# Hybrid backbone step on one core: gates' bias tile, early RWKV loads, token tiles to DRAM, and the order of the last attention units

## The chip, the cores and the metric

The kernel runs on one NeuronCore of a Trainium2 chip. The metric is device time of one execution in microseconds (us), lower is better. Time before: 2095.14 us, the median of 3 runs (2094.40 to 2097.18).

## The reference

One inference step of a two-layer backbone, for 256 prompt tokens and 1024 latent tokens that share the weights (model width 1024, 10 tiles of 128 tokens). Cut to what matters here:

```
h = rms_norm(x, g) * (1 + scale) + shift          # scale, shift, gate from SiLU(cond) @ mod_w + mod_b
layer 0: z = h @ w_in                              # 3584 columns
   A: q, k (normed, rotary), softmax attention: latents read 512 cached + 1024 own keys, prompt its own 256
   B: RWKV-7 scan, forward and backward, 8 heads of 64
   out = concat(A * silu(gate_a), (norm(B) + bonus) * silu(gate_b)) @ w_out
   x1 = x + gate * out
layer 1: z = h1 @ w_in -> gated linear attention (GLA), 4 heads, both directions
   y = final_norm(x1 + gate * (rms_norm(o) * silu(g)) @ w_out)
```

Products that need full precision are made of three products of rounded halves (high x high, high x low, low x high; `mm3`), so a tile of 128 tokens through the output projection is 2 halves of 512 columns with 24 products each.

## The kernel before, in words

The whole program is written by a planner, `Sched` (L104). Each piece of work is a Python generator, a task, that emits instructions with modelled costs; tasks come in streams, and `drive` (L411) takes at each step the instruction that could start earliest by the model, less the lead of its stream; on equal times the lower rank of the stream goes first, then the earlier task. The order that comes out is the order of each engine's queue on the chip, and each engine works its queue strictly in that order. Three details matter:

- A PE instruction that uses another size of the array than the one before it counts as 0.095 later (L296, `SWITCH`).
- A stream is given as (tasks, how many at once, share, lead, spare). With a share its rank begins at that of the RWKV stream and rises with the PE time that it has used; RWKV has share 2000, attention 150, the maxima 60 (L1793 to L1797).
- Buffers are counted slots: `get(tag)` waits until a slot of this name is free in the plan, `put` gives it back. `sch.until(...)` holds a task back in the plan; it makes no instruction.

All DMAs are issued on the SP queue.

Stages, in order of time:

1. *Layer-0 projections* (to about 510 us): `units`, `operands`, and eight gate units (`gated`, L785). A gate unit needs one of two `gt` buffers per group of tokens: PE's result, tanh on ACT, a product on DVE, a store to DRAM; then the buffer is free.
2. *Rooms.* SBUF is reused stage by stage. `room_attn` (L1239) opens the attention's tiles, loads the keys KA, and clears the lower half of both KB on GpSimd. `room_rwkv` (L1310) waits until the gate units are over and two PSUM banks are free, loads three masks, allocates and fills the RWKV tiles, and then sets the flag `rwkv`; only then do the segments (`rwkv_seg`, L1381) ask for their buffers and load AR, BK and Vs (three buffers each).
3. *Mixers* (about 515 to 1290): 40 RWKV segments, the attention in 12 units (p4, g): four pairs of heads times three groups of tokens, g = 0 the 256 prompt tokens (2 tiles of keys), g = 1 and 2 the 512 latents each (12 tiles of keys). The order of units is (1, 2, 0) for each p4 (L1668). `maxima` makes the row maxima of a unit ahead of it, at a pace tied to the units done (`want`, L1696), and writes them into row 64 of QB; `attend` makes the exponentials and the products with the values. `mods` (L1300) computes the remaining modulation columns with 1 MB of weights each; for the gate columns it takes a `gt` buffer for the bias row (`row` in `mod_cols`, L551, L565).
4. *Output projection of layer 0.* When all segments are over, `room_proj` (L2274) opens the output weights and two buffers each for `oh`, `ol` (halves of the input of a tile) and `xt`. `out_tile` (L2191) takes a tile of 128 tokens when all eight parts of its group's mixer output are in DRAM (four attention units, four RWKV norms): load through the single buffer `wst`, split, 48 products, gate, add to x, squares, store of x1 (L2256). It then waits for the flag `normed`, keeping its `xt`, and `norm_tile` (L621) scales `xt` in place, turns it with PE, and writes the layer-1 input. Order of tiles: groups 1, 2, 0. The gate row of a group is loaded into one buffer, which is free for the prompt's row when all eight latent tiles are over (L2214).
5. `room_norm` (L2281) sets `normed` when all 12 attention units, the modulation and the RWKV norms are over. Then the layer-1 projections may begin: `project` (L1805) loads weights through the same `wst` (`split_weights`, L655). Two gate units of layer 1 go first (`NGATE`); the GLA's rooms open when all ten tiles are normed.
6. *Layer 1*: projections, GLA, output projection (to 2093 us).

Of the kernel before, what the change touches and what calls it, by code (L numbers as in the profile page):

```python
# [20 lines left out]
P = 128  # L21
# [465 lines left out]
def tile_hybrid_dit_step(ctx: ExitStack, tc: tile.TileContext, I, C, O):  # L487
# [63 lines left out]
    def mod_cols(i, c0, n, bank, row, ready=lambda: True):  # L551
# [4 lines left out]
        for a in range(NK // nk):  # L556
            w = yield from get("mw", False)
            ws.append(w.rearrange("p a c -> p (a c)").rearrange("p (k c) -> p k c", c=n))
            D.dma_start(out=ws[a], in_=I["mod_w"][i, a * nk * P:(a + 1) * nk * P, c0:c0 + n].rearrange("(k p) c -> p k c", p=P))

            def loaded():
                mod_loads[0] += 1
            sch.then(loaded)
            if a == 0 and c0 >= 2 * DM:
                b = yield from get(row, False)  # L565
                D.dma_start(out=b[0:2, 0:n], in_=I["mod_b"][i:i + 1, c0:c0 + n].to_broadcast([2, n]))
# [9 lines left out]
        m4 = yield from get("m4", False)  # L576
        m = m4[:, 0:n]
        copy(m, p)
        if c0 < 2 * DM:
            k0 = c0 % DM // P  # L580
            ks = slice(k0, k0 + n // P)
            q = p[:, 0:2 * (n // P)].rearrange("p (k c) -> p k c", c=2)
            with sch.together():
                for k in range(n // P):
                    PE.matmul(q[:, k, :], lhsT=m[:, k * P:(k + 1) * P], rhs=msel, start=True, stop=True)
            wide = lambda r: par[:, r + ks.start:r + ks.stop].unsqueeze(2).to_broadcast([P, n // P, 2])
            to = gsh[i][:, 1 - c0 // DM, ks, :]
            V.tensor_tensor(to, q, wide(R_MB + i * 16 + c0 // DM * 8), ALU.add)
            if c0 >= DM:
                V.scalar_tensor_tensor(out=to, in0=to, scalar=1.0, in1=wide(R_NG + i * 8), op0=ALU.add, op1=ALU.mult)  # L590
        else:
            PE.matmul(p[0:2, :], lhsT=msel, rhs=m, start=True, stop=True)
            V.tensor_tensor(b[0:2, 0:n], p[0:2, :], b[0:2, 0:n], ALU.add)
            V.tensor_scalar(m[0:2, :], b[0:2, 0:n], 0.5, 0.0, ALU.mult, ALU.add)
            put(row, b)
            D.dma_start(out=gate_d[i][:, c0 - 2 * DM:c0 - 2 * DM + n], in_=m[0:2, :])
# [121 lines left out]
    flags = dict(left=0, gates=0, attn=False, keys=0, rwkv=False, mods=False, normed=False, gla=False, gl=False, units=0, weights=0, lr=0, begun=0, ra=False)  # L718
# [8 lines left out]
    shared("sq", 6, [P, 4])  # L727
# [12 lines left out]
    def layer0():  # L740
# [153 lines left out]
        def mods(n):  # L894

            yield from sch.until(lambda: loads[0] >= (5 if n % 2 else 1))
            yield from mod_cols(0, n * 512, 512, "a", "xr", lambda: modded[0] and modded[1])
# [341 lines left out]
    def room_attn():  # L1239
# [27 lines left out]
        for v in range(2):  # L1267
            G.memset(KB[v][64:128, :].bitcast(F32), 0.0)
            G.memset(KB[v][64:65, :].bitcast(F32), 1.0)
# [7 lines left out]
    def load_keys(v, x):  # L1277

        src = kh_d[64 * v:64 * v + 64, 0, :]
        if x == 0:  # L1280
            for h in range(2):
                D.dma_start(out=KA[v][64 * h:64 * h + 64, :].bitcast(F32), in_=kh_d[64 * v:64 * v + 64, h, :])
        else:
            D.dma_start(out=KB[v][0:64, :].bitcast(F32), in_=src)

    def keys():

        yield from sch.until(lambda: flags["attn"])
# [11 lines left out]
    def mods():  # L1300
        yield from sch.until(lambda: flags["attn"])
        for i, c0 in ((0, 2 * DM), (1, 0)):
            for c in range(c0, 3 * DM, 256):
                yield from mod_cols(i, c, 256, "b", "gt")
# [5 lines left out]
    def room_rwkv():  # L1310
# [15 lines left out]
        D.dma_start(out=m1f, in_=C["k_m1"].rearrange("p (d c) -> p d c", d=2))  # L1326
        id16 = rc.tile([P, P], F16, name="id16")
# [10 lines left out]
        slots("y", 2, [P, T], pool=rn)  # L1338
        slots("AR", 3, [P, 3, 4, 64])
        slots("BK", 3, [P, 2, 4, 64])  # L1340
        slots("Vs", 3, [P, 2, 2, 64])
# [326 lines left out]
    units = [(p4, g) for p4 in range(4) for g in (1, 2, 0)]  # L1668
# [120 lines left out]
    def attention(f):  # L1789
        for i, (p4, g) in enumerate(units):  # L1790
# [6 lines left out]
              (attention(attend), 2, 150), ([keys()], 1), ([mods()], 1))  # L1797
# [7 lines left out]
    def project(cols, use):  # L1805
        yield from sch.until(lambda: flags["normed"])
        yield from project_on(I["od_w_in"][0], H["hi"], H["lo"], cols, use, lambda g, a: normed[g] == GROUPS[g][1] // P, ORDER)
# [75 lines left out]
    def gates(h, u):  # L1883
# [13 lines left out]
        yield from project([(0, OD_G + unit * P, P)], use)  # L1897
# [293 lines left out]
    def out_tile(i, tt, src, finish):  # L2191
# [19 lines left out]
        put("wst", ot)  # L2211
        if i == 1:
# [7 lines left out]
        m = 256 if tt == 2 else 512  # L2220
# [30 lines left out]
    used = {}  # L2251
    NW1 = 2
    MIXED = (8, 4)

    def finish0(tt, xt, sq):
        D.dma_start(out=x1_d[tt], in_=xt)  # L2256
        yield from sch.until(lambda: flags["normed"])
# [4 lines left out]
        sch.then(done)  # L2262

# [10 lines left out]
    def room_proj():  # L2274
# [3 lines left out]
        slots_in(pool(left, "xr", side="left"))("xr", 1, [P, NK, P])  # L2278
# [75 lines left out]
    def tiles(i):  # L2354
        return ((out_tile(i, tt, (x_src, lambda t: x1_d[t])[i], (finish0, finish1)[i]) for tt in TILES), 3)

    def weights(i):
# [6 lines left out]
              weights(0), tiles(0), *gla, (projections(), 2, None, 0.0, 1.5), weights(1), tiles(1))  # L2364
# [85 lines left out]
```

## Time and profile before

| | us |
|---|---|
| median of 3 runs | 2095.14 |
| the profiled execution | 2095.28 |
| its span in the trace | 2093.5 |
| PE busy | 1997.0 (95%) |
| PE weight loads busy (beside the products) | 1557.7 (74%) |
| DVE busy | 1452.4 (69%) |
| ACT busy | 1007.6 (48%) |
| POOL (GpSimd) busy | 289.9 (14%) |
| DMA engines busy, mean share of the 16 | 33% |

The engine rows overlap in time; the span is the time from the first to the last instruction on the busiest path, and the run's time is 1.8 us more. Nearly every instruction carries line L357, the line of the planner that issues it, so instructions are told apart by the names of the tiles: `woh,oh` is a product of the output projection, `ident,xt` a transpose in `norm_tile`, `pt,VO` attention with the values, `QA,KA` and `QB,KB` scores, `KA,QA` maxima, `AR,BK` the first products of an RWKV segment. `pj` and `a` are PSUM banks. In brackets behind an instruction stands the time that its engine stood idle before it and what ended that.

### The profile page before, as it was taken

The numbers are of one execution on the slowest core, as the hardware profiler recorded it, in microseconds if no ns is written. First come the engines' busy times: TensorE is split into PE (matmuls) and PEld (weight loads), VectorE is DVE, ScalarE is ACT, GpSimd is POOL, SyncE is SP. The second block draws the span as 40 slices with busy tenths as digits, with TensorE's granted clock in tenths as the row PEclk, the third lists the DMA queues.
The fourth block names the chain that finished last, engine by engine and source line by source line (L and its number), as shares of the span: only waits on it lengthen the run. The fifth ranks groups of instructions, "written<-read, shape, count | busy, mean of one in ns | idle before, by whom it ended". The sixth has DMA issues, their size and how long they took to land.

```text
span 2093.5 us, 38539 instructions
## 1 busy us (share of the span) xinstructions
PE 1997.0 (95%) x14876; PEld 1557.7 (74%) x14876; DVE 1452.4 (69%) x2879; ACT 1007.6 (48%) x2184; POOL 289.9 (14%) x383
## 2 busy tenths in 40 slices
PE   6999999998999999999999999799999999999998
PEld 4878687886667777777776766578778888888886
DVE  4677866777887888778888987453575656564455
ACT  4454744553556655665656563333445454542111
POOL 2010200013221112121110020010121111110011
PEclk9999999999999999999999999899999999999999
DMA  8224342527513241323223224342102011115653
GB/s 297 71 101 159 138 164 81 179 91 238 170 54 103 81 143 59 97 74 111 78 68 88 67 70 143 95 146 73 50 14 64 28 50 29 49 31 165 192 170 112
DMA packets 215143, 219.56 MB, mean 105 GB/s; under 512 B 16480, under 2 KB 161232, under 8 KB 214960
## 3 DMA queue, kind: packets, MB, share of 16 engines
q1 hardware_dynamic: 214960, 217.10, 33.0%
q8 instruction: 117, 1.92, 0.4%
q14 instruction: 66, 0.54, 0.1%
HBM read 149.63 MB, written 67.39 MB: 104 GB/s over the span
## 4 chain that ended last, share of the span: by engine, by line
PE 52%; DVE 11%; issue 4%; ACT 3%; DMA 1%; POOL 0%; SPq 0%; POOLq 0%; DVEq 0%; ACTq 0%
PE a L357 26%; PE pj L357 26%; DVE QQ L357 2%; DVE LL L357 1%; DVE mx L357 1%; ACT QQ L357 1%; DVE TT L357 1%; DVE dec L357 1%; DVE gt L357 1%; DVE Z L357 1%; DVE y L357 1%; DVE GR L357 0%; DVE KX L357 0%; DVE GH L357 0%; DVE Ad L357 0%
## 5 line engine op out<-in xcount | busy, mean ns | idle before, releaser
L357 PE MATMUL pj<-hhi,whi 128*128 128x512 f32 (+1 forms) x672 | 241.1, 361 | 2.6 <-DVE whi L357 1.4
L357 PE MATMUL pj<-hhi,wlo 128*128 128x512 f32 (+1 forms) x672 | 240.4, 360 | 1.6 <-DVE wlo L357 1.6
L357 PE MATMUL pj<-hlo,whi 128*128 128x512 f32 (+1 forms) x672 | 241.3, 361 | 0.6 <-DVE hlo L357 0.6
L357 PEld LDWEIGHTS pj<-hhi,whi 128*128 128x128 f32 x672 | 128.9, 192 | 26.4 <-issue 3.7
L357 PEld LDWEIGHTS pj<-hhi,wlo 128*128 128x128 f32 x672 | 128.9, 192 | 24.0 <-issue 4.1
L357 PEld LDWEIGHTS pj<-hlo,whi 128*128 128x128 f32 x672 | 129.1, 192 | 23.7 <-issue 5.8
L357 POOL TENSOR_TENSOR acc<-acc,pt 128x512 f32<-128x512 f32 (+1 forms) x57 | 73.0, 1286 | 389.3 <-ACT pt L357 190.5
L357 PE MATMUL a<-h1hi,whi 128*128 128x512 f32 (+2 forms) x304 | 111.9, 369 | 0.0
L357 PE MATMUL a<-h1lo,whi 128*128 128x512 f32 (+2 forms) x304 | 111.0, 366 | 0.0
L357 PE MATMUL a<-h1hi,wlo 128*128 128x512 f32 (+1 forms) x296 | 109.9, 371 | 0.0
L357 PE MATMUL pj<-h1hi,whi 128*128 128x512 f32 (+2 forms) x296 | 108.4, 366 | 1.5 <-ACT h1hi L357 0.8
L357 PE MATMUL pj<-h1lo,whi 128*128 128x512 f32 (+2 forms) x296 | 108.4, 366 | 0.0
L357 PE MATMUL pj<-h1hi,wlo 128*128 128x512 f32 (+1 forms) x280 | 102.4, 366 | 0.0
L357 DVE TENSOR_TENSOR acc<-acc,pt 128x512 f32<-128x512 f32 (+1 forms) x127 | 90.6, 736 | 14.4 <-ACT pt L357 9.5
L357 PE MATMUL a<-pt,VO 128*64 128x512 f32 (+1 forms) x368 | 95.9, 605 | 0.0
L357 POOL TENSOR_SCALAR sq<-sq 128x1 f32<-128x1 f32 x70 | 19.9, 284 | 510.2 <-ACT gt L357 225.1
L357 DVE TENSOR_REDUCE mx<-pj 128x1 f32<-128x512 f32 (+1 forms) x118 | 75.4, 653 | 3.3 <-PE pj L357 3.1
L357 DVE TENSOR_REDUCE mx<-a 128x1 f32<-128x512 f32 x90 | 59.1, 669 | 10.8 <-PE a L357 10.7
L357 ACT ACTIVATE pt<-pj 128x512 f32<-128x512 f32 (+1 forms) x105 | 60.8, 597 | 10.2 <-PE pj L357 7.8
L357 PE MATMUL pj<-woh,oh 128*128 128x512 f32 (+1 forms) x160 | 61.5, 384 | 3.9 <-DVE oh L357 3.9
L357 PEld LDWEIGHTS a<-h1hi,whi 128*128 128x128 f32 (+1 forms) x304 | 56.9, 187 | 9.5 <-DVE gt L357 0.8
L357 PEld LDWEIGHTS pj<-h1hi,whi 128*128 128x128 f32 (+1 forms) x296 | 55.5, 188 | 11.2 <-ACT h1hi L357 1.2
(509 smaller groups left out, 5477.0 us busy)
## 6 DMA issues: line engine op xcount, KB each, us to landing
mw<-in_mod_w SPq DMA_DIRECT2D x24, 1024.0 KB
ws<-wk SPq DMA_DIRECT2D x32, 512.0 KB
wst<-in_ev_w_in SPq DMA_DIRECT2D x26, 512.0 KB
wst<-in_od_w_in SPq DMA_DIRECT2D x24, 512.0 KB
AR<-ws SPq DMA_DIRECT2D x40, 256.0 KB
BK<-ws SPq DMA_DIRECT2D x40, 256.0 KB
wst<-o SPq DMA_DIRECT2D x14, 512.0 KB
Vs<-vt SPq DMA_DIRECT2D x80, 64.0 KB
```

The lines of the kernel that those rows point to most:

```text
L357: r = f(*a, **k)
```

## The change

- `mod_cols` no longer takes a `gt` (or `xr`) buffer for the bias row: it takes `m4` earlier and puts the bias into its second half.
- `room_rwkv` allocates y, AR, BK and Vs ahead of the other RWKV tiles and sets a new flag `segs`; the segments load on `segs` and wait for `rwkv` only behind their loads. KB and VO (`keys`) are loaded after `segs`. The lower half of each KB is cleared on VectorE, where its upper half is loaded.
- The last pair of heads has the unit order (0, 1, 2), and the last two units are a stream of their own without share and with lead 0.15.
- Layer-0 token tiles go in the order 0 to 9 (prompt first). Tiles from 4 on wait ahead of their products until all steps of keys of all units are made. A tile that is over before `normed` gives its `xt` back after the store of x1; `renorm` loads x1 again later and norms it. `sq` has 12 slots in place of 6, `xr` 2 in place of 1.
- Layer-1 projections wait until eight token tiles have been split; the two early gate units take the groups in the order 0, 1, 2.

```diff
@@ mod_cols
             if a == 0 and c0 >= 2 * DM:
-                b = yield from get(row, False)
-                D.dma_start(out=b[0:2, 0:n], in_=I["mod_b"][i:i + 1, c0:c0 + n].to_broadcast([2, n]))
+                m4 = yield from get("m4", False)
+                b = m4[0:2, n:2 * n]
+                D.dma_start(out=b, in_=I["mod_b"][i:i + 1, c0:c0 + n].to_broadcast([2, n]))
...
@@ room_attn, load_keys, keys
         load_keys(0, 0)
-        for v in range(2):
-            G.memset(KB[v][64:128, :].bitcast(F32), 0.0)
-            G.memset(KB[v][64:65, :].bitcast(F32), 1.0)
...
         else:
+            V.memset(KB[v][64:128, :].bitcast(F32), 0.0)
+            V.memset(KB[v][64:65, :].bitcast(F32), 1.0)
             D.dma_start(out=KB[v][0:64, :].bitcast(F32), in_=src)
...
-        yield from sch.until(lambda: flags["attn"])
+        yield from sch.until(lambda: flags["attn"] and flags["segs"])
@@ room_rwkv, rwkv_seg
         D.dma_start(out=m1f, in_=C["k_m1"].rearrange("p (d c) -> p d c", d=2))
+        slots("y", 2, [P, T], pool=rn)
+        slots("AR", 3, [P, 3, 4, 64])
+        slots("BK", 3, [P, 2, 4, 64])
+        slots("Vs", 3, [P, 2, 2, 64])
+
+        def loads():
+            flags["segs"] = True
+        sch.then(loads)
...
-        yield from sch.until(lambda: flags["rwkv"])
+        yield from sch.until(lambda: flags["segs"])
...
+        yield from sch.until(lambda: flags["rwkv"])
         pair(AR[:, 2], id2.unsqueeze(1).to_broadcast([P, 4, 64]), last.to_broadcast([P, 4, 64]), ALU.mult)
@@ attention
-    units = [(p4, g) for p4 in range(4) for g in (1, 2, 0)]
+    units = [(p4, g) for p4 in range(4) for g in ((1, 2, 0) if p4 < 3 else (0, 1, 2))]
...
-              (attention(attend), 2, 150), ([keys()], 1), ([mods()], 1))
+              (attention(attend, 0, 10), 2, 150), (attention(attend, 10), 2, None, 0.15), ([keys()], 1), ([mods()], 1))
@@ project, gates
-    def project(cols, use):
-        yield from sch.until(lambda: flags["normed"])
...
+    def project(cols, use, order=ORDER):
+        yield from sch.until(lambda: flags["normed"] and split[0] >= 8)
...
-        yield from project([(0, OD_G + unit * P, P)], use)
+        yield from project([(0, OD_G + unit * P, P)], use, (0, 1, 2) if unit < NGATE else ORDER)
@@ out_tile
         put("wst", ot)
+
+        def got():
+            split[i] += 1
+        sch.then(got)
...
-        m = 256 if tt == 2 else 512
+        m = 256 if tt == 2 * i else 512
+
+        yield from sch.until(lambda: i == 1 or tt < 4 or attended[0] == sum(span(g)[3] for _, g in units))
@@ finish0
         D.dma_start(out=x1_d[tt], in_=xt)
-        yield from sch.until(lambda: flags["normed"])
+        if not flags["normed"]:
+            put("xt", xt)
+
+            def stored():
+                rest[tt] = sq
+            sch.then(stored)
+        else:
+            yield from norm0(tt, xt, sq)
+
+    def norm0(tt, xt, sq):
         yield from norm_tile(1, tt, xt, sq, H["hi"], H["lo"])
...
+    def renorm():
+
+        yield from sch.until(lambda: flags["normed"])
+        for tt in range(10):
+            yield from sch.until(lambda: tt in rest or normed[0 if tt < 2 else (tt + 2) // 4] == (2, 4, 4)[0 if tt < 2 else (tt + 2) // 4])
+            if tt in rest:
+                xt = yield from get("xt")
+                D.dma_start(out=xt, in_=x1_d[tt])
+                yield from norm0(tt, xt, rest[tt])
...
-        return ((out_tile(i, tt, (x_src, lambda t: x1_d[t])[i], (finish0, finish1)[i]) for tt in TILES), 3)
+        return ((out_tile(i, tt, (x_src, lambda t: x1_d[t])[i], (finish0, finish1)[i]) for tt in (range(10), TILES)[i]), 3)
...
-              weights(0), tiles(0), *gla, (projections(), 2, None, 0.0, 1.5), weights(1), tiles(1))
+              weights(0), tiles(0), ([renorm()], 1), *gla, (projections(), 2, None, 0.0, 1.5), weights(1), tiles(1))
```

## Rows read from the trace of the kernel before

**Rows 1.** The page's first part (span; busy time of each engine, its share of the span, its instructions).

```profile
span 2093.5 us, 38539 instructions
PE 1997.0 (95%) x14876; PEld 1557.7 (74%) x14876; DVE 1452.4 (69%) x2879; ACT 1007.6 (48%) x2184; POOL 289.9 (14%) x383
```

**Rows 2.** Busy time by stretch. Columns: stretch and its length (us), then for PE, PEld, DVE, ACT and POOL the busy time and (x) the number of instructions, then the granted PE clock, the mean busy share of the DMA engines and the GB/s that they moved.

```profile
500.00:515.00 15.00, 9.96 (x44) 7.95 (x43) 4.26 (x10) 1.07 (x2) 13.41 (x16) 0.93 0.92 250
515.00:530.00 15.00, 11.37 (x42) 6.54 (x41) 14.17 (x37) 4.53 (x13) 7.92 (x19) 0.73 0.88 266
530.00:545.00 15.00, 11.53 (x92) 8.04 (x91) 12.80 (x29) 5.72 (x13) 2.65 (x3) 0.77 0.90 281
...
560.00:1235.00 675.00, 659.32 (x7105) 493.07 (x7106) 566.72 (x1261) 405.14 (x998) 102.34 (x102) 1.00 0.27 82
...
1250.00:1270.00 20.00, 14.76 (x46) 7.08 (x47) 16.86 (x25) 10.88 (x17) 1.60 (x1) 0.85 0.74 209
...
1315.00:1350.00 35.00, 23.21 (x103) 15.81 (x102) 14.60 (x24) 17.28 (x40) 1.16 (x3) 0.80 0.34 106
1350.00:1410.00 60.00, 60.00 (x282) 50.02 (x281) 32.75 (x47) 20.45 (x47) 6.44 (x10) 1.00 0.43 138
1410.00:1420.00 10.00, 7.63 (x32) 5.96 (x31) 5.50 (x8) 4.78 (x10) 0.00 (x0) 0.83 0.37 84
```

**Rows 3.** The same view in slices of 5 us, for the slow stretches behind the attention.

```profile
1340.00:1345.00 5.00, 2.86 (x10) 2.07 (x10) 2.36 (x3) 2.50 (x8) 0.00 (x0) 0.50 0.55 144
1345.00:1350.00 5.00, 4.96 (x13) 3.70 (x13) 2.38 (x5) 0.91 (x3) 0.00 (x0) 0.58 0.53 172
...
1415.00:1420.00 5.00, 5.00 (x18) 3.98 (x18) 2.93 (x5) 3.31 (x7) 0.00 (x0) 0.75 0.64 130
```

**Rows 4.** The list of PE's instructions in order of time, from 510 to 540 us (start, time, engine, operation, out<-in, count, and in brackets the idle time before it and what ended it): the first product behind the projections, and the first one of an RWKV segment.

```profile
514.69 0.77 PE L357 MATMUL a<-KA,QA 128*128 128x512 f32 x1 [5.04 <-DMA QA<-qh]
...
534.56 0.58 PE L357 MATMUL a<-AR,BK 64*128 64x128 f32 x1
```

**Rows 5.** The list of the SP queue (all DMAs are issued there, in this order) from 505 to 540 us.

```profile
505.58 0.33 SPq L357 DMA_DIRECT2D gt<-in_mod_b  x1
...
509.54 0.59 SPq L357 DMA_DIRECT2D KB<-kh  x1
...
510.87 0.38 SPq L357 DMA_DIRECT2D gb<-gt  x1
...
517.42 0.53 SPq L357 DMA_DIRECT2D gmask<-in_k_gmask  x1
...
527.74 0.57 SPq L357 DMA_DIRECT2D AR<-ws  x1
```

**Rows 6.** The lists of ACT, POOL and DVE in the same stretch: the last gate tile's activation, the clearing of KB, the last clearing of the RWKV tiles on POOL, and a DVE instruction with one input of 512 columns.

```profile
520.30 0.60 ACT L357 ACTIVATE gt<-pj 128x512 f32<-128x512 f32 x1 [15.33 <-DMA gb<-gt]
502.07 6.43 POOL L357 MEMSET KB<- 64x1792 f32 x4
517.46 2.38 POOL L357 MEMSET Z<- 128x512 f16 x5
524.35 0.42 DVE L357 TENSOR_SCALAR LL<-ident 128x512 f32<-128x512 f32 x1
```

**Rows 7.** PE's instructions in order of time from 1260 to 1415 us, those with a wait before them and the first products of a token tile.

```profile
1260.61 0.27 PE L357 MATMUL pj<-ident,mx 128*4 128x128 f32 x1 [1.99 <-DVE mx L357]
1264.56 0.79 PE L357 MATMUL a<-QB,KB 128*128 128x512 f32 x1 [2.98 <-DMA QB<-mr]
...
1288.89 0.28 PE L357 MATMUL a<-woh,oh 128*128 128x256 f32 x1
...
1316.84 1.94 PE L357 MATMUL a<-pt,VO 128*64 128x512 f32 x8
1321.85 0.65 PE L357 MATMUL a<-acc,VO 128*64 128x256 f32 x4 [1.01 <-DVE rcp L357]
1326.02 0.66 PE L357 MATMUL pj<-ident,xt 128*128 128x128 f32 x4 [1.96 <-ACT xt L357]
...
1341.01 1.12 PE L357 MATMUL pj<-ident,xt 128*128 128x128 f32 x4 [7.50 <-DVE xt L357]
...
1412.84 0.66 PE L357 MATMUL pj<-ident,xt 128*128 128x128 f32 x4 [2.37 <-DVE xt L357]
```

**Rows 8.** The SP queue from 1285 to 1390 us, and the DVE instruction that frees the loading buffer `wst`.

```profile
1302.67 0.39 SPq L357 DMA_DIRECT2D wst<-in_od_w_in  x1
...
1339.25 0.53 SPq L357 DMA_DIRECT2D wst<-o  x1
...
1366.06 0.33 SPq L357 DMA_DIRECT2D xt<-in_x_sample  x1
...
1389.61 0.33 SPq L357 DMA_DIRECT2D xt<-in_x_sample  x1
1338.00 1.22 DVE L357 TENSOR_TENSOR wlo<-wst,whi 128x1024 fp32r<-128x1024 f32 x1
```

**Rows 9.** The chain of waits, in order of time (start, length, what): half a token tile of 48 products with what stands before it, and the store of a finished tile.

```profile
1352.46 10.88 PE a L357 x48
...
1406.49 5.42 DMA x<-xt
```

More of the change, by code (lines that the diff above doesn't have):

```diff
@@ L549, in tile_hybrid_dit_step, with mod_cols @@
     mod_loads = [0]
-    def mod_cols(i, c0, n, bank, row, ready=lambda: True):
+    def mod_cols(i, c0, n, bank, ready=lambda: True):
         nk = 2048 // n
@@ L575, in mod_cols @@
             put("mw", ws[ks[0] // nk])
-        m4 = yield from get("m4", False)
+        if c0 < 2 * DM:
+            m4 = yield from get("m4", False)
         m = m4[:, 0:n]
@@ L592, in mod_cols @@
             PE.matmul(p[0:2, :], lhsT=msel, rhs=m, start=True, stop=True)
-            V.tensor_tensor(b[0:2, 0:n], p[0:2, :], b[0:2, 0:n], ALU.add)
-            V.tensor_scalar(m[0:2, :], b[0:2, 0:n], 0.5, 0.0, ALU.mult, ALU.add)
-            put(row, b)
+            V.tensor_tensor(b, p[0:2, :], b, ALU.add)
+            V.tensor_scalar(m[0:2, :], b, 0.5, 0.0, ALU.mult, ALU.add)
             D.dma_start(out=gate_d[i][:, c0 - 2 * DM:c0 - 2 * DM + n], in_=m[0:2, :])
@@ L717, in tile_hybrid_dit_step @@
     left, segs, right = (ctx.enter_context(ExitStack()) for i in range(3))
-    flags = dict(left=0, gates=0, attn=False, keys=0, rwkv=False, mods=False, normed=False, gla=False, gl=False, units=0, weights=0, lr=0, begun=0, ra=False)
+    flags = dict(left=0, gates=0, attn=False, keys=0, rwkv=False, mods=False, normed=False, gla=False, gl=False, segs=False, units=0, weights=0, lr=0, begun=0, ra=False)
     def pool(stack, name, **k):
@@ L726, in tile_hybrid_dit_step @@
     shared("gt", 2, [P, 512])
-    shared("sq", 6, [P, 4])
+    shared("sq", 12, [P, 4])
     shared("pj", 4, [P, 512], pool=pp)
@@ L896, in mods @@
             yield from sch.until(lambda: loads[0] >= (5 if n % 2 else 1))
-            yield from mod_cols(0, n * 512, 512, "a", "xr", lambda: modded[0] and modded[1])
+            yield from mod_cols(0, n * 512, 512, "a", lambda: modded[0] and modded[1])
             def done():
@@ L1303, in mods @@
             for c in range(c0, 3 * DM, 256):
-                yield from mod_cols(i, c, 256, "b", "gt")
+                yield from mod_cols(i, c, 256, "b")
         def done():
@@ L1337, in room_rwkv @@
         V.tensor_tensor(id2, ident[:, 0:64], ident[:, 64:128], ALU.add)
[L1338 to L1341, printed above, removed]
         slots("BT", 2, [P, 4, P])
@@ L1788, in tile_hybrid_dit_step, with attention @@
     order = ((0, 1, 2, 3, 4), (0, 4, 3, 2, 1))
-    def attention(f):
-        for i, (p4, g) in enumerate(units):
+    def attention(f, a=0, b=12):
+        for i, (p4, g) in list(enumerate(units))[a:b]:
             yield f(i, p4, g)
@@ L1803, in tile_hybrid_dit_step @@
     c128 = "p (c t) -> p c t"
-    def project(cols, use):
-        yield from sch.until(lambda: flags["normed"])
-        yield from project_on(I["od_w_in"][0], H["hi"], H["lo"], cols, use, lambda g, a: normed[g] == GROUPS[g][1] // P, ORDER)
+    def project(cols, use, order=ORDER):
+        yield from sch.until(lambda: flags["normed"] and split[0] >= 8)
+        yield from project_on(I["od_w_in"][0], H["hi"], H["lo"], cols, use, lambda g, a: normed[g] == GROUPS[g][1] // P, order)
         def done():
@@ L2251, in tile_hybrid_dit_step @@
     used = {}
+    split = [0, 0]
+    rest = {}
     NW1 = 2
@@ L2277, in room_proj @@
         out_pool(0, left, "wo0", 2)
-        slots_in(pool(left, "xr", side="left"))("xr", 1, [P, NK, P])
+        slots_in(pool(left, "xr", side="left"))("xr", 2, [P, NK, P])
         yield from move("b", "pj", 3)
```

## The prediction

> **What bounds the kernel now.** I began with the page's first part [rows 1]: PE is busy for 1997.0 of 2093.5 us, so 96.5 us of the span can go at all while PE's work stays as it is, and this change leaves PE's products as they are. The next view is the busy time by stretch [rows 2]; look there for stretches in which PE's busy time is under the length, or its clock under 1.00. Three matter here. At the start of the mixers (515 to 545) PE is busy 11.37 and 11.53 of 15 us at clocks of 0.73 and 0.77. The long middle (560 to 1235) is nearly full: 659.32 of 675 us. Around the end of the attention, 1250 to 1270 has 14.76 of 20 us, 1315 to 1350 has 23.21 of 35 at 0.80, 1410 to 1420 has 7.63 of 10 at 0.83. After that come the lists by engine, to see which wait ends last in each.
>
> The start: PE ends the projections and waits 5.04 us for QA, and the first RWKV product comes only at 534.56 [rows 4]. The RWKV loads are issued at 527.74, behind KB and everything else; the gate store that stands behind KB in the SP queue goes out at 510.87 [rows 5], and the last gate tile's activation sits 15.33 us until such a store has landed, because one of the two `gt` buffers was given to the modulation's bias at 505.58 [rows 5, 6]. Its PSUM bank is what room_rwkv waits for.
>
> The end: the first token tile's products run at 1288.89. The last products of unit (3, 2) follow only at 1316.84, behind two whole tiles: they use 64 columns of the array where the tiles use 128, and the planner adds 0.095 for such a switch, so a token product always looks earlier. Only then comes the short unit (3, 0), with waits of 1.01 and 1.96, and then 7.50 us before the transposes of 1341.01 [rows 7]. That last one is the single loading buffer: the layer-1 weights took `wst` at 1302.67, DVE frees it with the subtraction at 1338.00, and the next token tile is loaded at 1339.25 [rows 8].
>
> **The change part by part.** I sum against the profiled execution, 2095.28 us (span 2093.5 and 1.8 around it); the median of the runs is 2095.14, so nothing has to be shifted.
>
> *Gates' own tiles and the early RWKV loads (the start).* With both `gt` left to the gates, the last activation can follow its last product: PE is done at 514.69 - 5.04 = 509.65 [rows 4], so about 510 in place of 520.30, and gmask's load (517.42, [rows 5]) goes out near 512. The RWKV loads then come right behind the three mask loads. What is issued there: for three segments AR, BK and two Vs, by their shapes 256 + 256 + 2 x 64 KB, 1.9 MB in all, 7 us at the 266 to 281 GB/s of these stretches [rows 2], where the queue is 0.88 to 0.90 busy. They pass KB (448 KB by its shape), VO (896 KB) and some of the modulation's 1 MB weight loads; KB and VO come up to 7 us later, which costs nothing as long as the attention's products start where they did, behind QB's row of maxima. The clearing of POOL's tiles ends at 517.46 + 2.38 = 519.84 [rows 6] and is not moved; with the copies behind it, RWKV can begin near 523, 11.5 us before 534.56.
> How much of that is time? Lost in 515 to 545 are 7.1 us of idle PE and, at 0.73 and 0.77, another 11.37 x 0.27 + 11.53 x 0.23 = 5.7: 12.8 us, the upper bound. But DVE is busy 14.17 and 12.80 of the 30 us [rows 2]: 3.0 us free. It also gets KB's clearing, 6.43 us on POOL for four [rows 6]; on DVE I take 1792/512 x 0.42 = 1.5 us each from the row of 512 columns, so 3 us now and 3 us when the second KB is loaded, where PE is covered by RWKV. If the first two fall among the maxima, they cost 3 us: the lower bound is -3. If they fall into DVE's idle time before 515 (4.26 of 15 busy), nothing. I take a gain of 4, near what DVE had free plus part of the clock.
>
> The Trainium skill, page "Perfetto Trace Analysis", section "Identifying the Most-Contended Engine", says that the busy share of the products is a poor measure of TensorE's distance from its limit, and that the share of LDWEIGHTS should be read. By it the middle stretch is not full: 493.07/675 = 73%, against 50.02/60 = 83% in 1350 to 1410 [rows 2], and a start 11.5 us earlier would carry through whole; the sum would be 2070. The trace of before can't settle it: the same stretch has the 73% and only 15.7 us in which no product runs.
>
> *The attention's last units first.* Their stream gets a lead of 0.15, more than the 0.095 of the switch, so the products of 1316.84 would follow their exponentials and not two tiles. With (3, 0) before (3, 1), its latency lies under other work. From 1315 to 1350 the idle is 35 - 23.21 = 11.8 us; 7.50 and about 1.1 more belong to `wst`, so 3.2 belong to this; all of it goes, as the held tiles are there to fill. Count 3. The waits of 1.99 and 2.98 at 1260 [rows 7] stand at the border between the last two big units, which stays. The pace of the maxima runs one step of keys further ahead there (the short unit counts 1.0 in the pace and 2 in steps, 2 us): between 0 and 5.0, I take 1.
>
> *Token tiles held back, weights of layer 1 later.* projections wait for eight splits, so `wst` isn't taken: 7.50 + 1.1 go, and with them the slow clock behind the wait, 2.86 x 0.50 + 4.96 x 0.42 = 3.5 [rows 3]; 12.1 in all. Next late there is the store of x1, in place of which the scaled tile is written: 5.42 us [rows 9], seen as 2.37 at 1412.84 [rows 7]. I leave that much standing: 10 gained. The hold for tiles from 4 on is a wait in the planner and blocks no engine; until it ends the attention's products and tiles 0 to 3 (10.88 us each, [rows 9]) feed PE. It also delays nothing, as token tiles can't start before the last RWKV norm, near 1289 in both orders. What the weights' wait takes away is the filling by two gate units between 1350 and 1410; tiles alone must then keep PE full. Two loads of `xt` that use the same buffer are 23.6 us apart (1366.06 and 1389.61, [rows 8]), 11.8 per tile, about 10.88 and the transposes: balanced, without room.
>
> *Prompt tiles first.* The change of gate row, now at 1410 to 1420 (2.37 idle and 5.00 x 0.25 = 1.25 of clock, [rows 2, 3]), moves to between tiles 1 and 2; half of 3.6, so 1.5 with something kept, taken between 0 and 3.6.
>
> *x1 to DRAM and back.* Each tile finished before the norm's room is open is stored (it was before), and now read back, 512 KB, about the 5.42 us of its store. Starting at 1289, with the room open near 1300, that is one or two tiles. Each holds one of the two `xt` for a load, a scaling and the transposes. Hidden it costs 0; if PE stands before its transposes as at 1341.01, 7.50 each. Two tiles: 0 to 15, I take 2.
>
> *At nothing:* twelve `sq` and two `xr` (space only); the bias in m4 (its load waits for the former column's gate store, but the 1 MB of weights before it takes longer); the short chunks in tile 0 instead of 2.
>
> Sum: 4 + 3 + 1 + 10 + 1.5 - 2 = 17.5, so 2095.3 - 17.5 = 2078.
>
> **The rivals.**
> *A, the shift carries through.* RWKV has the first rank in the middle, and if its chain rather than PE's total sets the end, 11.5 us come in place of 4: 2070. For it: DVE is at 566.72 of 675, nothing is full but PE. Against it: PE has only 15.7 us idle there.
> *B, only the end works.* DVE, full from 515 on, keeps the start where it was: 2078 + 4 = 2082.
> *C, the change doesn't do what it says.* The planner puts products by modelled times; with another order of loads the whole middle is laid out anew, and if the attention ends as late against RWKV as now, tiles 0 to 3 are used up before it and the gap of 1315 to 1350 returns with 1410's. Of the gains 1.5 stay: 2094.
> *D, the other side: the reloads.* PE takes its instructions in order. A transpose placed by the modelled landing of a reload stands in front of products that could run. If the room opens late, four tiles or more are stored and read back, through two `xt` that have no room: each 7.50, 4 x 7.50 = 30 in place of 2, so 2078 + 28 = 2106. It decides from three reloads on: 17.5 + 2 - 7.5 x 3 is below 0. For it: 23.6 us per pair of tiles. Against it: with the lead the room should open after one or two.
>
> **How the numbers follow.** The forecast 0.48 (its own range 2070 to 2087, from 12.8 or -3 at the start and 0 to 15 for the reloads, not all at once), A 0.13, B 0.13, C 0.13, D 0.13. A measurement of this kernel can tell 0.2%, 4.2 us, from no change. Faster (below 2091): forecast, A and B, 0.74; within: C, 0.13; slower: D, 0.13. The range runs from 2066, a little under A, to 2097, past C, and leaves out D and the far edge of A.
>
> **What would show it.** Gates: the last gate activation near 510, AR's load near 513, the first AR,BK product before 526; 515 to 545 with more than 25 us of PE. End: no pause of token products inside the last attention unit, the layer-1 weights loaded after the eighth token tile, at most two reloads of x1, no PE wait over 4 us between the attention's end and the last norm. I am wrong if the gap stays with another name (a store or a reload of x1 before the transposes), or if the middle, 560 to the last RWKV step, grows by more than 4 us.

## The result, and the profile after

The changed kernel takes 2106.05 us (median, 2102.66 to 2107.85); the kernel before, on the same chip, 2094.6. The ratio is 1.0052, 95% interval [1.0039, 1.0065]: slower by 0.5%, some 11 us, where 17 us less was forecast. The profiled execution took 2104.78 us. Its page begins so, to be held against [rows 1]:

```profile
span 2103.0 us, 38559 instructions
PE 2001.8 (95%) x14876; PEld 1565.0 (74%) x14876; DVE 1461.2 (69%) x2868; ACT 1009.8 (48%) x2190; POOL 283.9 (13%) x388
```

The products are the same 14876. Of the 9.5 us of longer span, 4.7 are idle time of PE (2103.0 - 2001.8 = 101.2 against 96.5) and 4.8 are products that take longer; the mean granted clock of the run is lower as well (0.975 against 0.984). Busy time by stretch, columns as in [rows 2]:

```profile
515.00:530.00 15.00, 7.79 (x28) 3.68 (x26) 14.13 (x15) 3.75 (x11) 10.72 (x29) 0.61 1.01 334
530.00:545.00 15.00, 10.98 (x99) 8.10 (x96) 11.94 (x30) 6.48 (x15) 1.04 (x1) 0.61 0.57 140
560.00:1235.00 675.00, 659.61 (x7144) 495.04 (x7146) 567.82 (x1250) 405.27 (x1012) 111.82 (x113) 1.00 0.30 89
1250.00:1270.00 20.00, 19.96 (x77) 8.99 (x75) 19.79 (x29) 12.15 (x22) 2.72 (x1) 1.00 0.52 161
1315.00:1350.00 35.00, 33.00 (x142) 21.62 (x142) 17.80 (x28) 11.80 (x23) 1.49 (x4) 1.00 0.22 76
1350.00:1410.00 60.00, 57.61 (x266) 44.37 (x263) 33.34 (x50) 26.10 (x56) 3.66 (x8) 1.00 0.37 120
1410.00:1420.00 10.00, 10.00 (x50) 8.37 (x49) 5.66 (x9) 3.42 (x9) 0.00 (x0) 1.00 0.48 110
1420.00:1450.00 30.00, 23.37 (x136) 20.19 (x136) 16.87 (x32) 18.93 (x45) 1.48 (x4) 0.89 0.35 105
```

The stretches that were to gain at the end did: 1250 to 1270, 1315 to 1350 and 1410 to 1420 are nearly full. But the loss came back behind them (1350 to 1410 and 1420 to 1450), and the start, meant to be fuller, is emptier: 515 to 545 has 18.77 us of products at a clock of 0.61, against 22.90 at 0.73 and 0.77. The kernel before has 1420 to 1450 full:

```profile
1420.00:1450.00 30.00, 30.00 (x142) 24.99 (x141) 8.99 (x14) 8.29 (x20) 1.48 (x4) 1.00 0.13 52
```

To put a number on a stretch I add, over its slices of 5 us, the idle time and the busy time times (1 - clock). In this table and below, the slices are the same view as above:

| stretch (us) | before | after | difference | forecast |
|---|---|---|---|---|
| 500 to 600 | 19.5 | 32.7 | +13.2 | -4 |
| 600 to 1200 | 16.4 | 10.9 | -5.5 | 0 |
| 1200 to 1480 | 29.8 | 30.8 | +1.0 | -13.5 |
| 1480 to the end | 19.1 | 17.7 | -1.4 | 0 |

That is 7.3 of the 9.5 us. (Products of one kind stand in other slices in the two kernels, so a line of the table is good to a few us. It is also no measure of time where something else than PE sets the pace: up to 500 PE works the same products in the same order in both kernels and the measure has 9.5 us more in the changed one, mostly from a clock of 0.83 and 0.76 against 1.00 and 0.93 in the first 50 us, but its first maxima product comes at 514.47 against 514.69.)

**The start.** DVE and POOL of the changed kernel, in order of time; the columns are those of [rows 6]:

```profile
514.30 5.64 DVE L357 COPY Z<-id 128x256 f16<-128x256 f16 x2 [2.27 <-POOL Z L357]
519.86 0.41 DVE L357 TENSOR_SCALAR LL<-ident 128x512 f32<-128x512 f32 x1
520.68 1.55 DVE L357 MEMSET KB<- 64x1792 f32 x1 [0.41 <-issue]
522.67 1.55 DVE L357 MEMSET KB<- 1x1792 f32 x1 [0.43 <-DVE KB L357]
524.25 0.69 DVE L357 TENSOR_REDUCE mx<-a 128x1 f32<-128x512 f32 x1
...
513.29 2.38 POOL L357 MEMSET Z<- 128x512 f16 x5
515.62 1.84 POOL L357 MEMSET LL<- 128x1024 f32 x2
517.41 2.39 POOL L357 MEMSET Z<- 128x512 f16 x5
```

And DVE of the kernel before:

```profile
515.49 0.69 DVE L357 TENSOR_REDUCE mx<-a 128x1 f32<-128x512 f32 x1 [7.84 <-PE a L357]
...
524.08 0.35 DVE L357 COPY Z<-id 128x256 f16<-128x256 f16 x2
```

Two such copies take 0.35 us before and 5.64 after: before, they came when POOL had done clearing; after, they stand among the clears and end at 519.94, just behind the last clear (519.80). Behind them stand KB's two clears, and only then the first row of maxima, at 524.25 in place of 515.49. PE shows it as one wait, and RWKV's first product, forecast for 523, comes at 532.77:

```profile
525.00 0.80 PE L357 MATMUL a<-KA,QA 128*128 128x512 f32 x1 [7.21 <-DVE mx L357]
...
532.77 0.58 PE L357 MATMUL a<-AR,BK 64*128 64x128 f32 x1
```

The attention pays most. Its first product with the values runs at 587.5 (before: 546.4), half of them are done at 1042.0 (1002.0), the last at 1356.7 (1322.3), while RWKV's last product of its chain of states comes at 1226 (1242). RWKV runs further ahead, and the attention is left behind it. A late first product is not the whole of it: KB and VO are now loaded behind the RWKV loads, and in the best version of the start (s_both, below), which is faster than the kernel before, that product still comes at 578.0, but half of them are done at 1009.6 and the last at 1319.

**The end.** PE in order of time: `mx` are the maxima of unit (3, 2), then its first and its last products, and the transposes of the last three tiles:

```profile
1302.40 0.27 PE L357 MATMUL a<-ident,mx 128*4 128x128 f32 x1
...
1330.74 0.27 PE L357 MATMUL a<-ident,mx 128*4 128x128 f32 x1
1330.76 0.48 PE L357 MATMUL pj<-QA,KA 128*128 128x512 f32 x1
...
1356.68 1.08 PE L357 MATMUL a<-pt,VO 128*64 128x512 f32 x4
...
1433.75 0.66 PE L357 MATMUL pj<-ident,xt 128*128 128x128 f32 x4 [1.09 <-ACT xt L357]
...
1441.50 1.09 PE L357 MATMUL a<-ident,xt 128*128 128x128 f32 x8 [1.63 <-DVE xt L357]
1443.52 1.09 PE L357 MATMUL pj<-ident,xt 128*128 128x128 f32 x4 [0.93 <-DVE xt L357]
```

Unit (3, 1) is through at 1265; the products of tiles 0 and 1 run from 1275 on, and the last unit's maxima trickle in between until 1330.74. The lead that the change gives holds for a unit's products, not for its maxima. So the attention ends late, the norm's room opens late, and four tiles are stored and read back (the last row holds two loads, issued 7.0 us apart):

```profile
1336.44 0.32 SPq L357 DMA_DIRECT2D xt<-x  x1
1404.13 0.33 SPq L357 DMA_DIRECT2D xt<-x  x1
1427.91 7.33 SPq L357 DMA_DIRECT2D xt<-x  x2
```

Of the three transposes, the first (1.09) and the last (0.93) are of tiles read back; the middle one (1.63) is of the last tile, which was kept in place and whose scaling stood 5.35 us behind its own store. With 3.00 us before the next product of layer 1 (`h1hi`, at 1448.46), that is the 6.6 us of idle time in 1420 to 1450.

### The profile page after: what moved, and what is told of

The parts are those of the page before. It is cut to its first block, busy times and chain, and to the rows that moved or that the text cites. A ratio compares the mean times of both kernels' runs of the same rounds, so it can differ in the third digit from the quotient of the medians.

```text
span 2103.0 us, 38559 instructions
## 1 busy us (share of the span) xinstructions
PE 2001.8 (95%) x14876; PEld 1565.0 (74%) x14876; DVE 1461.2 (69%) x2868; ACT 1009.8 (48%) x2190; POOL 283.9 (13%) x388
## 5 line engine op out<-in xcount | busy, mean ns | idle before, releaser
L357 PE MATMUL pj<-h1hi,whi 128*128 128x512 f32 (+3 forms) x440 | 162.5, 371 | 3.0 <-ACT h1hi L357 3.0
L357 PE MATMUL pj<-h1lo,whi 128*128 128x512 f32 (+3 forms) x440 | 161.0, 367 | 0.0
L357 PE MATMUL pj<-h1hi,wlo 128*128 128x512 f32 (+1 forms) x424 | 157.5, 372 | 0.0
L357 DVE TENSOR_TENSOR acc<-acc,pt 128x512 f32<-128x512 f32 (+1 forms) x133 | 94.8, 742 | 20.7 <-ACT pt L357 13.5
L357 PE MATMUL pj<-woh,ol 128*128 128x512 f32 (+1 forms) x264 | 99.4, 376 | 3.1 <-DVE ol L357 3.1
L357 PE MATMUL pj<-woh,oh 128*128 128x512 f32 (+1 forms) x264 | 99.6, 377 | 2.8 <-DVE oh L357 2.8
L357 PE MATMUL pj<-wol,oh 128*128 128x512 f32 (+1 forms) x264 | 99.1, 375 | 0.0
L357 PEld LDWEIGHTS pj<-h1lo,whi 128*128 128x128 f32 (+1 forms) x440 | 82.7, 188 | 12.9
L357 PEld LDWEIGHTS pj<-h1hi,wlo 128*128 128x128 f32 x424 | 80.5, 190 | 11.5
L357 ACT ACTIVATE pt<-a 128x512 f32<-128x512 f32 (+1 forms) x98 | 56.2, 593 | 21.9 <-PE a L357 21.0
L357 DVE TENSOR_REDUCE mx<-a 128x1 f32<-128x512 f32 (+1 forms) x99 | 64.2, 667 | 1.4 <-PE a L357 1.0
```

The source lines that it names most:

```text
L357: r = f(*a, **k)
```

## The experiments

All times are of one core, with the kernel before run beside each on the same chip; since its median lay between 2093.5 and 2095.9, I compare ratios, and 0.001 is 2.1 us. My theory was: the start costs what the middle and the end can't give back, by the copies beside POOL's clears and KB's clears on DVE, and the attention then lags; the end's parts give nothing because the last unit's maxima have no lead. The rival: the end's parts (hold, weights' wait, reloads) are what makes it slower.

### The two halves alone

The kernel before with the start's hunks of the diff alone, and the changed kernel without them.

> The kernel before with the start's parts alone (gates' own tiles, early RWKV loads, keys behind them, KB's clearing on DVE). Theory: the start is what costs. In the changed kernel 500 to 600 lost 32.7 us of PE against 19.5, and the middle gave 5.6 back; so +5 to +13 on the kernel before, 2100 to 2108, with two copies of some 5 us beside POOL's clears and two KB clears of 1.55 us on DVE in the trace. Rival (the end's parts cost, the start is the gain I forecast): 2083 to 2093.

> The changed kernel with the start's parts undone (what is left: the last units' order and lead, the hold for tiles from 4 on, the later layer-1 weights, the reloads of x1). Theory (the start costs some 8, the end about nothing by itself): 2090 to 2098, fewer reloads than four, as the attention is no longer a unit behind RWKV. Rival (the end's parts cost): 2101 to 2110. My forecast's own terms for the end, 13.5 us, would give 2082.

Start alone 2106.33 us, 1.0061 [1.0048, 1.0074]; end alone 2096.59, 1.0014 [1.0004, 1.0024]. So the start costs 12.8 us by itself, and the end, forecast to give 13.5, is 2.9 slower. The rival, by which the end costs most, falls. The two halves don't add up: 15.7 alone, 10.9 together.

### KB's clearing

Back to where it was, on POOL, ahead of the other clears; in the changed kernel (e_kbpool) and in the start alone (s_pool):

```
+        for v in range(2):
+            G.memset(KB[v][64:128, :].bitcast(F32), 0.0)
+            G.memset(KB[v][64:65, :].bitcast(F32), 1.0)
...
-            V.memset(KB[v][64:128, :].bitcast(F32), 0.0)
-            V.memset(KB[v][64:65, :].bitcast(F32), 1.0)
```

> The changed kernel with KB's clearing back on POOL ahead of the other clears. Theory: the two DVE clears of 1.55 us stood in the path of the attention's maxima, and DVE is the engine that paces the start: 3 to 5 us faster than the changed kernel, 2100 to 2103, PE wait at 525 (7.2 us) shorter by 3. Rival (the blocked copies and the slow clock alone make the start's loss, and 6.4 us more of clears on POOL block DVE's copies the longer): 2104 to 2109.

> The start's parts on the kernel before, but with KB's clearing left on POOL. Theory: KB's clearing on DVE costs the same 7 to 8 us here as in the changed kernel (2106.3 for all of the start's parts, so 2097 to 2101), and what is left above the kernel before is the lock between POOL's clears and the copies. Rival (in this kernel the early loads cost, not KB): 2103 to 2108.

2098.48 us, 1.0026 [1.0016, 1.0035], against 1.0052: 5.4 us. And 2095.11, 0.9999 [0.9989, 1.001], against 1.0061: 13.0 us, more than theory gave. Two instructions of 1.55 us (and two more when KB is loaded the second time) cost up to four times the 3.1 us of the first pair.

The first row of maxima, which stands behind the first pair, explains a part only. With KB on POOL it comes 3.4 us earlier in the changed kernel (520.84 against 524.25) and 1.8 us in the start alone (521.27 against 523.09). Up to 775 us PE works the same products in the same order with KB on either engine, and with KB on DVE it is then 4.4 and 6.3 us late. From there, where DVE clears KB the second time (777.1 and 803.2 in the changed kernel), the planner's order is another one, and half of the attention's products are done 27 and 29 us later (1042.0 against 1014.9, 1043.8 against 1014.8). So about half of the 13.0 us arises only behind the second pair. Whether the clears themselves or the new order cost it, no run separates.

### The copies beside POOL's clears

All copies into the tiles that POOL clears forced to ACT:

```
-        V.tensor_copy(id16, ident)
+        S.copy(id16, ident)
...
-                linear(x[:, :, 0, :], ident.unsqueeze(1).to_broadcast([P, 4, P]), -1.0)
+                S.mul(x[:, :, 0, :], ident.unsqueeze(1).to_broadcast([P, 4, P]), -1.0)
...
-                    copy(fv(x[:, 0, d * h:d * h + 1], [[P, 4], [2 * h, 64 // h], [1, h]]),
+                    S.copy(fv(x[:, 0, d * h:d * h + 1], [[P, 4], [2 * h, 64 // h], [1, h]]),
```

> The changed kernel with the copies into POOL's freshly cleared tiles (Z, the diagonal of LL, id16) all on ACT, so that DVE copies nothing beside POOL's clears; KB's clearing stays on DVE. Theory (a DVE copy stands still as long as POOL clears, 5.64 us for two of 0.24): no DVE instruction over 2 us between 505 and 525, KB's clears and the first maxima 4 to 5 us earlier (reduce_max from about 520 in place of 524.25), and 3 to 6 us off the changed kernel: 2100 to 2103. Rival (the two copies had waited for POOL's tiles anyway, and what paces the start is POOL's clears or the loads): within 2 us, 2104 to 2108.

> Both mends of the start at once: KB's clearing on POOL and the copies on ACT. Theory: the two add up, since both free the same engine ahead of the maxima: 7.5 (measured for KB alone) and 3 to 6 more, 2092 to 2097. Rival (once KB is off DVE the next thing late is the loads of QA, AR and BK, which the trace has landing near 520): 2097 to 2101, no better than KB alone.

> The kernel before with nothing but the copies on ACT. Theory (before the change DVE's copies came after POOL's clears or between them, none over 1 us, so nothing is to be gained): within 3 us of before, 2092 to 2098. Rival (the copies cost as much there): 2087 to 2091.

Alone in the changed kernel: 2103.96 us, 1.0039 [1.0024, 1.0053], which its interval can't tell from the changed kernel's. DVE's list shows why:

```profile
512.24 1.55 DVE L357 MEMSET KB<- 64x1792 f32 x1 [0.43 <-issue]
513.83 6.75 DVE L357 COPY ring<-id 64x64 f32<-64x64 f32 x3
521.01 1.55 DVE L357 MEMSET KB<- 1x1792 f32 x1 [0.43 <-DVE ring L357]
522.59 0.69 DVE L357 TENSOR_REDUCE mx<-a 128x1 f32<-128x512 f32 x1
```

With the Z copies gone, the planner put three other copies there, for `ring`, and they stood among the clears for 6.75 us: the lock (so I call it when a copy stands still beside POOL's clears) found another victim, so my expectation that no DVE instruction would last over 2 us failed. It does show that copies into a tile that POOL isn't clearing are held as well. A DVE memset isn't: 1.55 us at 512.24, beside POOL's clears, as at 520.68 in the changed kernel, after them. With KB on POOL as well (e_kbz), nine ring copies stand beside the same clears and get through one clear at a time, in 3.18 us together (the last section has them), and the first maxima stand almost where the kernel before has them:

```profile
511.90 3.18 DVE L357 COPY ring<-id 64x64 f32<-64x64 f32 x9
516.08 0.69 DVE L357 TENSOR_REDUCE mx<-a 128x1 f32<-128x512 f32 x1 [1.01 <-PE a L357]
```

2093.32 us, 0.9988 [0.9977, 0.9999], 8.0 us under KB on POOL alone, by ratios; PE's products come in the same order in these two kernels, so here the copies alone are what differs. In the kernel before, the copies on ACT change nothing that can be told: 2094.2, 0.9994 [0.9985, 1.0002]. There the late gate tile had kept the copies behind the clears.

### The start without its two costs, and the gates alone

> The start's parts on the kernel before with both mends: KB's clearing on POOL and the copies on ACT. My forecast's gain for the start, 4 us, was made without the two costs, so with them gone it should appear: 2087 to 2092 (the changed kernel gained 5 to 8 from the copies once KB was off DVE). Rival (an earlier start doesn't carry through, as RWKV then only runs further ahead of the attention): 2093 to 2098.

> The kernel before with the gates' own tiles alone: the modulation's bias goes into m4, the RWKV loads stay behind the tables, KB's clearing stays on POOL. My forecast: the last gate activation near 510 in place of 520.30, and some 4 us gained, 2089 to 2093. Theory of the lock: POOL's clears move forward with the gates and DVE copies stand beside them, so most of what the gates give is lost again: 2093 to 2099, with a DVE instruction over 3 us between 505 and 525.

> The gates' own tiles alone (2123.3 us) and the copies on ACT. Theory (a good part of the 27 us is the lock, which moves the first maxima, and with them the attention, behind RWKV): 2100 to 2112, attention's end nearer to 1324 than to 1348. Rival (without the early loads the order of the middle is bad by itself): 2116 to 2125.

With both mends the start's parts on the kernel before give 2091.75 us, 0.9979 [0.9969, 0.9988]: 4.4 us gained, where my sum had 4. The gates' own tiles alone, with the RWKV loads left where they were, gave a surprise: 2123.29, 1.0137 [1.012, 1.0154], 29 us slower. The lock is part of it (again 5.63 us for two Z copies, at 516.11), but with the copies on ACT it is still 2117.1, 1.0107 [1.0094, 1.012]: 6 us of the 29, and the rest as the rival had it. Forecast and theory both missed this kernel. The traces show the same lag as in the changed kernel, larger: RWKV's last chain product at 1231 and 1228 (before 1242), the attention's last at 1349 and 1345 (before 1322), and then all the waits of [rows 7] behind the attention, 7.50 among them. With the early loads added (s_both), the attention ends at 1319. Why the loads' place turns the order of the middle like that is not settled.

### The leads at the end

First a lead for the maxima of the last two units (the first of them also waits until the unit before has its queries), then also for the RWKV norms; both in the changed kernel, with its costly start, and both leads on the end's parts alone (e_endlead).

```
-              (attention(maxima), 1, 60),
+              (attention(maxima, 0, 10), 1, 60), (attention(maxima, 10), 1, None, 0.15),
...
-    mixers = (((rwkv_norm(p, sts[p]) for p in range(4)), 1),
+    mixers = (((rwkv_norm(p, sts[p]) for p in range(4)), 1, None, 0.15),
```

> The changed kernel with the lead of 0.15 also for the maxima of the last two units, not for their products alone. Theory: the last unit's maxima were starved behind the products of tiles 0 and 1 (1275 to 1331); with the lead unit (3, 2) runs some 25 us earlier, the attention ends near 1335 instead of 1361, at most two tiles are stored and reloaded, and the tail is better filled: 2096 to 2101. Rival (where the last unit stands doesn't matter as long as tiles fill PE; the end's loss is the tail without gate products): within 2 us of the changed kernel, 2104 to 2108.

> The changed kernel with the lead for the last maxima and also a lead of 0.15 for the RWKV norms, so that the last norm's sums don't stand behind the leading attention. Theory: with the lead for the maxima alone the last norm's sums came at 1300 to 1303, after the whole attention, and the first token tile waited 16.27 us for its input; with the norm first, tile 0 is ready before the attention ends, the stall of 16.27 goes, and so 12 to 20 us off that run: 2097 to 2105. Rival (the norm is late because of its own loads and its ACT and DVE steps, or the second wait, 10.76 us for xt, only moves): 2110 to 2117.

> The end's parts alone (2096.6 us) with the leads for the last maxima and the norms, and the start as in the kernel before. Theory (the end's parts gave nothing because the last unit's maxima stood alone on PE, 1255 to 1280, with DVE's reductions between them): 2087 to 2092. Rival (the leads only repair what the earlier start broke): 2094 to 2099.

The first was a miss: 2116.57 us, 1.011 [1.0097, 1.0123]. The attention did end early, at 1303 in place of 1358, but nothing was ready to follow. PE's list:

```profile
1300.39 1.02 PE L357 MATMUL pj<-gsq,bones 128*128 128x512 f32 x2
...
1319.55 0.58 PE L357 MATMUL pj<-woh,oh 128*128 128x256 f32 x1 [16.27 <-DVE oh L357]
...
1357.27 1.11 PE L357 MATMUL pj<-ident,xt 128*128 128x128 f32 x4 [10.76 <-DVE xt L357]
```

The `bones` products are the last RWKV norm's sums. They stood behind the leading attention until 1300, and token tiles need the normed rows. With a lead for the norms too, those sums come by 1260, the 16.27 us go, and the time is 2095.82, 1.0007 [0.9996, 1.0019], 21.6 us less. On the end's parts alone the two leads give 2087.78, 0.9969 [0.9956, 0.9982], against 1.0014: 9.4 us. So the end's parts fail by themselves, not only behind the changed start. Without the leads the maxima of the last unit stood nearly alone on PE, with DVE's reductions between them; the trace of the end alone shows them from 1254 to 1281, with waits of 2.52, 3.45 and 2.01 us.

### Everything together, and two terms of the end

> Everything at once: KB's clearing on POOL, the copies on ACT, the leads for the last maxima and for the norms. Theory: start as before the change or better (gain of 10 on the changed kernel), end without the late unit (gain of 2 to 8): 2088 to 2096. Rival (the middle is laid out anew with each change and gives the gains back): 2097 to 2106.

2087.88 us, 0.9958 [0.9945, 0.9972]: 8.8 us under the kernel before, where the mended start alone gives 4.4 and the end's parts with both leads 6.5. From it, two single edits: the layer-1 weights no longer wait for eight splits, and the normalized tile is written to a buffer of its own, in the place of the second `xr`.

```
-        yield from sch.until(lambda: flags["normed"] and split[0] >= 8)
+        yield from sch.until(lambda: flags["normed"])
...
-        linear(xt, xt, sq[:, 2:3])
+            linear(ys, xt, sq[:, 2:3])
```

> The version with everything mended (KB on POOL, copies on ACT, leads for the last maxima and the norms), without the wait of layer 1's weights for eight splits. My forecast's term (the single loading buffer is worth some 10 us): 2093 to 2100 against 2088. Rival (a stall of 7 us stands before the second transposes in either case, now for x1's store, so the buffer is worth little): 2085 to 2091.

> The version with everything mended, and the normalized tile written to a buffer of its own (a second xr's place), so that the scaling doesn't wait until x1's store has landed. Theory (the 6.9 us before the second transposes, 1322 to 1329, hang on the store of x1 issued at 1324.25): the scaling starts 2 to 3 us earlier, and the stall goes down to about 4; 2083 to 2087. Rival (square, rstd and scaling alone are as long, or with one xr the next norm is held up): 2086 to 2092.

Without the weights' wait 2092.66, 0.9983 [0.9973, 0.9994]: it is worth 5.2 us, half of my 10. (That may be too much: of the 4.4 us between the two profiled executions, 2.4 stand there already at the attention's last product, 1296.8 against 1299.2, before this wait can act.) With the extra buffer 2086.68, 0.9961 [0.9946, 0.9975], the same as without. The rows are the second tile's transposes with the wait before them: first everything together, then without the weights' wait, then with the extra buffer.

```profile
1328.89 1.12 PE L357 MATMUL pj<-ident,xt 128*128 128x128 f32 x4 [6.94 <-DVE xt L357]
```

```profile
1333.50 1.12 PE L357 MATMUL pj<-ident,xt 128*128 128x128 f32 x4 [10.19 <-DVE xt L357]
```

```profile
1327.38 1.08 PE L357 MATMUL pj<-ident,xs 128*128 128x128 f32 x4 [5.87 <-DVE xs L357]
```

The gap of 7.50 us in [rows 7] is 6.94 with the buffer free and x1's store in front of the scaling, and 5.87 with that gone too. What is left is the tile's own chain (last sum, square, its root, scaling) with nothing placed beside it. The hold for tiles from 4 on has no such run: with the leads, the planner writes the same program with and without it, as the tiles begin only when the attention ends.

## Why the prediction was wrong

**The start's term (+4, bounds -3 to 12.8).** The steps in time held as far as the queue: the last gate activation was at 509.54 (forecast 510), the AR load at 514.28 (513). Two steps behind it failed. The first: the clearing of POOL's tiles ends at 519.84 "and is not moved; with the copies behind it, RWKV can begin near 523". The copies moved in front of DVE's maxima and into the clears, where they cost 5.64 us. I had looked at when POOL is done, not at what DVE would do meanwhile; in the kernel before, DVE did the maxima in just that time. The second: KB's clearing at its duration, 3 us "if the first two fall among the maxima". They fell in front of them, and the pair for the second KB, which I had "covered by RWKV", is where the planner's order changes and the attention falls behind RWKV. Together they cost 5.4 us in the changed kernel and 13.0 in the start alone. So my lower bound of -3 was far too near: the start alone measures -12.8. With both costs gone the term has the size I gave it, 4.4 measured and 4 said; by which path it comes is not shown, since RWKV's chain starts 12.4 us earlier there and most of that is lost again on the way.

**The last units first (+3 and +1).** The failed step is the lead of 0.15, by which "the products of 1316.84 would follow their exponentials". They do: only four token products stand ahead of the last products of the unit, at 1355.65 to 1356.35. But a unit begins with its maxima, which have the ordinary rank, so the pause moved from within the unit to in front of it. With leads for the maxima and the norms, the end's parts gain 6.5 us on the kernel before; without, nothing.

**Tiles held, weights later (+10).** The weights are loaded after the eighth split, as said (1385.01), and 1315 to 1350 is full. The size was off: 5.2 us, perhaps less. The failed step is the reading of the 7.50 us as the wait for `wst`, "7.50 + 1.1 go": with the buffer free, 6.94 us stand before the same transposes, and 10.19 with it taken. I had put 2.37 there, for the store of x1; the store is about 1 of the 6.94, the rest is the tile's own chain.

**Reloads (-2, one or two tiles).** There were four, as rival D said, and its 2106 is the time measured, but that is luck. D's price was 7.50 us for each; the waits at reloaded tiles are 1.09 and 0.93 us. In the kernels with both leads no tile is read back at all. Its count was right since its condition was: the room opened late. That condition is rival C's (the attention as late against RWKV as before; in fact its last product came 34 us later), and C had no price for a start that loses.

**What held.** The gate row's change between tiles 1 and 2: 1410 to 1420 is full. No PE wait over 4 us between the attention's end and the last norm: the longest was 3.00. The middle did not grow; it lost 5.5 us less than before. Rival A, the start's shift carried through whole, is refuted: in s_both RWKV's first product of its chain comes 12.4 us earlier and 4.4 us arrive.

## What to carry to other kernels

When a wait goes, ask what it had kept apart: the late gate tile had kept DVE's copies out of POOL's clears, and no row of the kernel before could show the price. Price an instruction moved to another engine by what queues behind it there and by the order that the planner then makes, not by its duration. And a priority given to one stage of a pipeline has to be given to the stages that feed it, and to whatever feeds the work that is to follow, or the wait only changes its place.

## What the runs showed of the hardware

A DVE copy that starts while POOL clears one tile after another can be held not for one clear but to the end of the train: the two Z copies of the changed kernel took 5.57 and 4.71 us, against 0.35 for two such before, and two small ring copies of e_zact 6.41 and 6.34, against 0.19 before. It need not be so: in e_kbz nine ring copies beside the same clears got through, two or three behind each clear, in 0.42 to 1.04 us, and the clears beside them took up to 0.60 us in place of 0.52. The same is seen in s_both and in everything together. What decides between the two is not shown. The view by tile has the durations (shortest, median and longest, in ns), first of the changed kernel, then of e_kbz:

```profile
L357 DVE COPY Z<-id x2: 4705/5140/5574, 514.3 to 515.2; 128x256 f16<-128x256 f16 x2
```

```profile
L357 DVE COPY ring<-id x9: 424/852/1041, 511.9 to 514.7; 64x64 f32<-64x64 f32 x9
L357 POOL MEMSET Z<- x10: 517/518/601, 513.9 to 520.1; 128x512 f16 x10
```

DVE's maxima beside the same clears (515.49, 0.69 us) and its memsets (1.55) kept their duration, and ACT's copies of the same tiles took 0.39 to 0.41 us each. The Trainium skill, page "SBUF — State Buffer", section "Who interferes with whom", says that DVE's copies, casts and tensor_scalar in their two-port modes share a port pair with GpSimd, that whoever issues first has it for the whole instruction while the other fully blocks, and that reductions on trn2 don't contend. The traces agree for copies, for a cast (0.78 us in the changed kernel, 0.22 before) and for the maxima; no row here has a tensor_scalar beside the clears. Read for one instruction, the rule lets a copy wait for the clear that is running, as seen in e_kbz; in the changed kernel the copies were held through some ten clears. Had this rule been weighed in the prediction, the copies could have been a rival with a place.
